# A matmul-tanh-multiply kernel: the loads of w's last column block are released by another cast

## The chip, the cores and the metric

One Trainium2 chip, one of its cores. The metric is the device time of one launch in microseconds (us). A profile of one execution is at hand for the kernel before: its span runs from the first to the last instruction of the program, and its own time is a little longer than the span.

## The reference

```python
batch, m, k, n = 16, 512, 1024, 768      # x: 16x512x1024, w1 and w2: 1024x768, all float32
y1 = np.matmul(x, w1)
y2 = np.matmul(x, w2)
return (np.tanh(y1) * y2).astype(np.float32)
```

## The kernel before

**Tiling.** The 8192 rows of x make 64 row tiles of 128 (called mt, 0 to 63). The contraction over 1024 is eight slices k of 128. The 2 x 768 columns of w1 and w2 are cut into three blocks of 512: block a is w1's first 512 columns, block g holds the last 256 columns of w1 and of w2 side by side, and block b is w2's first 512 columns. Every operand is float16 on TensorE (PE), accumulated in float32 in eight PSUM banks.

**Stages.** Row tiles 0 to 3, the head, are multiplied plainly: one matmul of 128x512 for each row tile, block and k (line 434, `mm`, operations m0a0 to m3b7; those of row tile 3 and block b are kept for the very end). The other 60 row tiles go in 20 triples, with a scheme that does with 15 products of four matmuls each (line 457, `product`, operations p0.i to p14.i of triple i) what would plainly take more, and that needs sums of pieces of w (line 416, `w_sum`, operations B5 to B48, on VectorE, DVE) and of x (line 425, `x_sum`, operations S3.i to S63.i, on DVE). The sums of w are made once, while the head is multiplied. Results leave PSUM through tanh on ScalarE (ACT) and a multiply on DVE (thg0 to thg3 and mug0 to mug3 for block g of the head).

**How w comes in.** Block a and block g are loaded as float32 into slots of `arena` (operations La0 to La7, and Lg00 to Lg31: two halves for each pair of k) and cast to float16 in `wh`: a by DVE (ca0 to ca7), g by ACT (cg0 to cg7; line 372 and 370, `copy`). Lg20 and Lg21 bring what cg2 and cg6 cast, Lg30 and Lg31 what cg3 and cg7 cast. All g loads are issued on SP's queue (q1 in the profile). Block b is loaded by POOL's queue (q0, line 363), which turns float32 into float16 on the way and needs no cast; these eight operations are cb0, cb4, cb1, cb5, cb2, cb6, cb3, cb7, in this order. Behind them on POOL come the loads of the row tiles 6, 4, 5, then 7, 8, 9 and so on (line 366, `load_x`, operations L6, L4, L5, L7 ...). Only eight of POOL's loads can be under way by their semaphores: the ninth, L6, waits until cb0 has landed, L4 until cb4 has, and so on.

**What sets the order.** A small planner inside the kernel (class `Planner`) is given every operation with its engines, an assumed duration, what it needs and a due time, and a list `lands` of times at which loads are assumed to land. It plays the program through once and writes down the order in which each engine shall issue its operations. That order is fixed in the program: an engine that meets an operation whose input is not there yet waits, and all that stands behind it on the engine waits too. The planner's times have no other effect. `lands` comes from `shared_landings`, which lets the queues (`rings`) share the bandwidth in equal parts from the moments given in the list.

**The gate.** POOL's first operation after its start-up is a copy of one column of a cast slice (line 497, `gate`). It does nothing but wait for that cast; the b loads stand behind it.

```python
    GATE = ("g", 0)
    ...
    op("gate", {"pool": 0.1}, 0.0, ["c%s%d" % GATE], gate, *GATE)
    for n, what in enumerate(late):
        op(f"c{what}", {"pool": 0.58}, 0.1 * n, [], load_w, "b", int(what[1]), issued=[f"c{late[n - 1]}" if n else "gate"], lands=lands[what])
```

Of the kernel before, what the change touches and what calls it, by code (L numbers as in the profile page):

```python
# [74 lines left out]
class Planner:  # L75
# [9 lines left out]
    def op(self, name, engines, due, needs, fn, *args, behind=(), issued=(), chains=(), xfer=0.0, latency=None, seeds=False,  # L85
           lands=None, hold=0.0):
        assert name not in self.ops, name
        self.ops[name] = dict(engines=engines, due=due, needs=[n for n in needs if n], behind=[n for n in behind if n], issued=[n for n in issued if n], fn=fn, args=args,
                              chains=chains, xfer=xfer, latency=latency, seeds=seeds, lands=lands, hold=hold)
        for c in chains:  # L90
            self.chains.setdefault(c, {"left": 0, "bank": None, "end": 0.0, "act": 0.0, "dve": 0.0})["left"] += 1
# [134 lines left out]
def shared_landings(rings, start, latency):  # L226
    now, left, place, landed = start, {}, [0] * len(rings), {}
    while any(p < len(r) for p, r in zip(place, rings)):
        active = [j for j, r in enumerate(rings) if place[j] < len(r) and r[place[j]][1] <= now]
        waiting = [r[place[j]][1] for j, r in enumerate(rings) if place[j] < len(r) and r[place[j]][1] > now]  # L230
        if not active:
            now = min(waiting)
            continue
        step = min([left.get(j, rings[j][place[j]][2]) * len(active) for j in active] + [t - now for t in waiting])
        now += step
        for j in active:
            left[j] = left.get(j, rings[j][place[j]][2]) - step / len(active)
            if left[j] < 1e-6:
                landed[rings[j][place[j]][0]] = now + latency[j]
                place[j] += 1  # L240
                del left[j]
    return landed
# [3 lines left out]
def kernel(  # L246
# [266 lines left out]
    for n, p in enumerate(LAST_ORDER.split()):  # L513
# [5 lines left out]
    XW, XX = 0.655, 1.4  # L519
    on_sp = "x00 x10 x20 x30 x01 x11 a4 a5 x21 a6 x31 a7".split() + [f"g{k}{t}" for k in range(KH) for t in range(2)]  # L520
    late = [f"b{k}" for s, k in slices if s == "b"]
    rows_in = (HEAD + 2, HEAD, HEAD + 1)
    GATE = ("g", 0)
    rings = [[(n, 0.75 + 0.3 * j, 0.75 if n[0] == "g" else 0.81 if n in ("x10", "x20", "x30") else XW) for j, n in enumerate(on_sp)],
             [(f"a{k}", 0.75 + 0.45 * k, 0.81 if k else XW) for k in range(4)], [(n, 17.6 + 0.6 * j, 0.66) for j, n in enumerate(late)] + [(f"x{mt}", 22.0 + 0.6 * j, XX) for j, mt in enumerate(rows_in)]]
    lands = shared_landings(rings, 1.0, (2.1, 2.1, 2.6))

    for k in range(4):
# [1 line left out]
    for n, what in enumerate(on_sp):  # L530
# [3 lines left out]
        else:  # L534
            s, k = what[0], int(what[1])
            j = slices.index((s, k))
            old = [slices[i - SLOTS] for i in range(j, j + 1 + (s == "g")) if i >= SLOTS]
            op(f"L{what}", {"sp": 0.05}, 0.1 * n - 100, [], load_w, s, k, int(what[2]) if s == "g" else None, issued=before,
               behind=[f"c{a}{b}" for a, b in old], lands=lands[what])
    op("gate", {"pool": 0.1}, 0.0, ["c%s%d" % GATE], gate, *GATE)  # L540
    for n, what in enumerate(late):
# [12 lines left out]
    for t in range(2):  # L554
        for k in range(KO):
            late = START + 32 + 8 * (t * KO + k)
# [61 lines left out]
    mt = HEAD - 1  # L618
# [57 lines left out]
    for i in range(TRIPLES):  # L676
# [10 lines left out]
        for o in C_OPS:  # L687
# [19 lines left out]
            mt = HEAD + 3 * i + r  # L707
            due = soonest[i, name] + LAST
            if kind in ("t", "th"):
                lo, n = (0, F) if kind == "t" else (F, G)  # L710
                op(f"{name}.{i}", {"act": 0.5 if n == F else 0.285}, due, needs, c_tanh, i, r, o[4], lo, n, o[5],
                   behind=reuse_out(mt) + ([f"{FIRST_READER[name]}.{i}"] if i == TRIPLES - 1 and name in FIRST_READER else []), chains=chains)
            else:
                lo, n, at = (0, F, 0) if kind == "m" else (F, G, G)
                op(f"{name}.{i}", {"dve": 0.6 if n == F else 0.335}, due + 1, needs, c_mul, i, r, o[4], lo, n, at, chains=chains)
                outs[mt].insert(0 if kind == "m" else 1, f"{name}.{i}")
    for mt in range(MT):
# [7 lines left out]
        late = [f"{('p0', 'p4', 'p12')[(mt - HEAD) % 3]}.{i + 1}"] if i < TRIPLES - 2 else []  # L725
# [144 lines left out]
```

## Time and profile before

| | us |
|---|---|
| median of three runs | 298.97 |
| the three runs | 298.97, 302.17, 298.88 |
| the profiled execution's own time | 299.0 |
| its span | 297.2 |
| PE busy in the span | 289.5 (97%) |
| DVE busy | 254.9 (86%) |
| ACT busy | 226.1 (76%) |
| POOL busy | 51.7 (17%) |

The profile's rows give for each group or moment the engine, the line of the kernel, the operation, the tile written and the tiles read. A share of the whole span says little here: the head of the kernel, some 33 us, is another program than the 20 triples after it, so the time is read by windows and by the timeline of each engine. A matmul of 128x512 is listed with 379 ns, but such matmuls are pipelined and follow each other in about 0.216 us, as the starts in the timeline show.

### The profile page before, as it was taken

How to read it: one execution, taken by the hardware profiler on the slowest of the kernel's cores; microseconds unless marked ns; L12 is line 12 of the kernel's file. 1: busy time of each engine (PE TensorE's matmuls, PEld its weight loads, DVE VectorE, ACT ScalarE, POOL GpSimd, SP SyncE). 2: the span in 40 equal slices, each digit the busy share in tenths (PEclk: the TensorE clock that was granted, in tenths of full speed). 3: DMA queues.
4: the chain of work that ended last, by engine and by line, in shares of the span. 5: the costliest groups of instructions: out<-in, count | busy, mean ns of one | idle time of the engine just before them, and what ended most of it. 6: DMA issues, size and time to landing. Idle time of an engine off the chain costs nothing. (4 is left out here: it accounts for less than half of the span.)

```text
span 297.2 us, 4671 instructions
## 1 busy us (share of the span) xinstructions
PE 289.5 (97%) x1385; PEld 133.4 (45%) x1385; DVE 254.9 (86%) x539; ACT 226.1 (76%) x454; POOL 51.7 (17%) x129
## 2 busy tenths in 40 slices
PE   7999999999999999999999999999999999999993
PEld 5444444444444444444444444444444444444442
DVE  1669999989999998979989899889889898988884
ACT  3577899699878879797797988768686776868451
POOL 0064036030112210303122121122020200000000
PEclk9999999999999999999999999999999999999999
DMA  6999999999999999999999999999999999741234
GB/s 230 387 298 198 173 158 216 192 166 197 193 238 217 252 228 270 270 171 306 183 220 199 226 292 218 283 278 251 165 279 113 271 85 270 229 161 52 108 140 164
DMA packets 84427, 63.51 MB, mean 214 GB/s; under 512 B 62768, under 2 KB 66608, under 8 KB 84400
## 3 DMA queue, kind: packets, MB, share of 16 engines
q1 hardware_dynamic: 73456, 44.71, 64.0%
q0 software_dynamic: 9792, 16.78, 38.0%
q10 hardware_dynamic: 1152, 1.70, 1.6%
q8 instruction: 11, 0.18, 0.3%
q14 instruction: 16, 0.13, 0.1%
HBM read 39.85 MB, written 25.17 MB: 219 GB/s over the span
## 5 line engine op out<-in xcount | busy, mean ns | idle before, releaser
L457 PE MATMUL bank<-b,early_x 128*128 128x512 f16 x640 | 148.3, 379 | 0.1
L457 PEld LDWEIGHTS <-early_x 128*128 128x128 f16 x800 | 78.2, 98 | 95.1 <-issue 0.7
L461 ACT ACTIVATE arena<-bank 128x512 f32<-128x512 f32 x100 | 59.1, 596 | 33.4 <-PE bank L457 33.3
L467 DVE TENSOR_TENSOR bank<-bank,arena 128x512 f32<-128x512 f32 x100 | 69.6, 696 | 15.5 <-ACT arena L461 7.3
L475 DVE TENSOR_TENSOR o<-o,bank 128x256 f32<-128x256 f32 (+1 forms) x120 | 63.2, 547 | 5.8 <-ACT o L470 5.5
L394 ACT ACTIVATE junk<-xh 128x1024 f16<-128x1024 f16 x60 | 63.3, 1055 | 0.1
L457 PEld LDWEIGHTS <-xT 128*128 128x128 f16 x400 | 39.0, 98 | 46.4
L457 PE MATMUL bank<-b,xT 128*128 128x512 f16 x240 | 58.3, 379 | 0.0
L494 POOL CAST held<-xT 128x1 f32<-128x1 f16 x54 | 15.1, 280 | 163.7 <-DMA xT<-xh 163.7
L470 ACT ACTIVATE o<-bank 128x256 f32<-128x256 f32 (+1 forms) x80 | 34.4, 437 | 12.0 <-DVE bank L467 7.1
L457 PE MATMUL bank<-wh,xT 128*128 128x512 f16 x160 | 41.1, 379 | 0.0
L457 PE MATMUL bank<-wh,early_x 128*128 128x512 f16 x160 | 40.9, 379 | 0.0
L366 POOL DMA_DIRECT2D xh<-in_x_dram x60 | 31.7, 528 | 16.0 <-issue 5.4
L425 DVE TENSOR_TENSOR early_x<-early_x,xT 128x512 f16<-128x512 f16 x80 | 33.5, 418 | 0.6
L461 ACT ACTIVATE bank<-bank 128x512 f32<-128x512 f32 x40 | 21.5, 575 | 7.2 <-DVE bank L467 6.6
L470 ACT ACTIVATE o<-arena 128x512 f32<-128x512 f32 x40 | 25.1, 627 | 1.0 <-DVE arena L467 1.0
L434 PE MATMUL bank<-wh,xT 128*128 128x512 f16 x72 | 18.4, 379 | 1.1 <-DVE wh L372 0.5
L425 DVE TENSOR_TENSOR early_x<-xT,early_x 128x512 f16<-128x512 f16 x40 | 16.7, 418 | 0.0
L425 DVE TENSOR_TENSOR early_x<-xT,xT 128x512 f16<-128x512 f16 x40 | 16.7, 417 | 0.0
L467 DVE TENSOR_TENSOR bank<-arena,bank 128x512 f32<-128x512 f32 x20 | 13.9, 695 | 3.2 <-ACT o L470 1.7
L467 DVE TENSOR_TENSOR arena<-bank,arena 128x512 f32<-128x512 f32 x20 | 13.7, 685 | 1.4 <-ACT arena L461 1.3
L467 DVE TENSOR_TENSOR arena<-arena,bank 128x512 f32<-128x512 f32 x20 | 13.6, 678 | 0.0
(49 smaller groups left out, 135.4 us busy)
## 6 DMA issues: line engine op xcount, KB each, us to landing
out_dram<-o SPq DMA_DIRECT2D x60, 384.0 KB, 5.4
xh<-in_x_dram POOLq DMA_DIRECT2D x60, 256.0 KB, 6.7
arena<-in_w_dram SPq DMA_DIRECT2D x12, 256.0 KB, 5.5
early_x<-in_x_dram SPq DMA_DIRECT2D x8, 256.0 KB, 5.0
arena<-in_w_dram ACTq DMA_DIRECT2D x4, 256.0 KB, 5.9
wh<-in_w_dram POOLq DMA_DIRECT2D x8, 128.0 KB, 5.7
xT<-xh SPq DMA_TRANSPOSE x57, 6.6
out_dram<-o SPq DMA_DIRECT2D x2, 256.0 KB, 2.8
```

Of the source, the lines that this page charges most:

```text
L366: pin(nc.gpsimd.dma_start(xh(mt), xf[mt]))
L394: pin(nc.scalar.activation(junk[:, :src.shape[-1]], src, ACT.Abs, scale=scale, accum_out=sums[:, column:column + 1]))
L425: pin(engine[e].tensor_tensor(x_operand(i, v), x_operand(i, a), x_operand(i, b), OP[how]))
L434: pin(nc.tensor.matmul(bank(chain)[:, :rhs.shape[-1]], xt(mt)[:, k, :], rhs, start=first, stop=k == KO - 1, skip_group_check=True))
L457: pin(nc.tensor.matmul(place(i, dst), x_operand(i, a)[:, k, :], w_rhs(b, k), start=begins and k == 0, stop=k == KH - 1, skip_group_check=T ...
L461: pin(nc.scalar.activation(place(i, dst), place(i, src), ACT.Copy, scale=float(sign)))
L467: pin(nc.vector.tensor_tensor(place(i, dst), a, b, ALU.add if signs == (1, 1) else ALU.subtract))
L470: pin(nc.scalar.activation(out_tile(HEAD + 3 * i + r)[:, lo:lo + n], place(i, src)[:, :n], ACT.Tanh, scale=float(sign)))
L475: pin(nc.vector.tensor_tensor(o, o, place(i, src)[:, at:at + n], ALU.mult))
L494: pin(nc.gpsimd.tensor_copy(held, xt(mt)[:, 0, :1]))
```

## The change

The gate copies a column of the last slice of block a (cast by DVE) where it copied a column of the first slice of block g (cast by ACT), so POOL may issue the loads of block b once that earlier cast is done. In the list of assumed landings the first b load moves from 17.6 to 16.0, so that the planner takes the b slices as landing earlier and the last g slices as landing later.

```diff
-    GATE = ("g", 0)
+    GATE = ("a", 7)
     rings = [[(n, 0.75 + 0.3 * j, 0.75 if n[0] == "g" else 0.81 if n in ("x10", "x20", "x30") else XW) for j, n in enumerate(on_sp)],
-             ... [(n, 17.6 + 0.6 * j, 0.66) for j, n in enumerate(late)] + ...
+             ... [(n, 16.0 + 0.6 * j, 0.66) for j, n in enumerate(late)] + ...
     lands = shared_landings(rings, 1.0, (2.1, 2.1, 2.6))
```

The order that the planner writes changes with it. On PE, from the 17th matmul of block g on:

```
before: ... m3g1 m3g5 | m0g2 m0g6 m1g2 m1g6 m2g2 m2g6 m3g2 m3g6 | m0b0 | m0g3 m1g3 m0g7 m1g7 m2g3 m2g7 m3g3 m3g7 | m1b0 m2b0 | b4 x3 | b1 x3 | m0b5 ...
after:  ... m3g1 m3g5 | m0b0 m1b0 m2b0 | m0g2 m1g2 m0g6 m1g6 m2g2 m2g6 m3g2 m3g6 | b4 x3 | b1 x3 | m0g3 m1g3 m0g7 m1g7 m2g3 m2g7 m3g3 m3g7 | m0b5 ...
```

From m0b5 on PE's order is the same in both. On ACT, the tanh of rows 2 and 3 (block a) go ahead of cg2 and cg6, and the absolute sums D1 and D2 go ahead of cg3 and of thg0. On DVE the sums of w are dealt out anew: after B45.2 comes B6.0, then B5.3, B24.0, B36.3, B26.0, mug0 to mug3, B24.2, B37.3, B26.2, B18.0, B18.2, B6.2, B29.0; the second half of B29 moves from before S3.0 to behind S3.1. A few operations of ACT and DVE up to the third triple change places too; behind them the order is the same on every engine. No operation is added or taken away.

More of the change, by code (lines that the diff above doesn't have):

```diff
@@ L522 @@
     rows_in = (HEAD + 2, HEAD, HEAD + 1)
-    GATE = ("g", 0)
+    GATE = ("a", 7)
     rings = [[(n, 0.75 + 0.3 * j, 0.75 if n[0] == "g" else 0.81 if n in ("x10", "x20", "x30") else XW) for j, n in enumerate(on_sp)],
-             [(f"a{k}", 0.75 + 0.45 * k, 0.81 if k else XW) for k in range(4)], [(n, 17.6 + 0.6 * j, 0.66) for j, n in enumerate(late)] + [(f"x{mt}", 22.0 + 0.6 * j, XX) for j, mt in enumerate(rows_in)]]
+             [(f"a{k}", 0.75 + 0.45 * k, 0.81 if k else XW) for k in range(4)], [(n, 16.0 + 0.6 * j, 0.66) for j, n in enumerate(late)] + [(f"x{mt}", 22.0 + 0.6 * j, XX) for j, mt in enumerate(rows_in)]]
     lands = shared_landings(rings, 1.0, (2.1, 2.1, 2.6))
```

## The prediction

> **What bounds the kernel now.** First, where PE, the busiest engine, has idle time: a table of stretches of the span, each row with the busy time and count of PE, PEld, DVE, ACT and POOL, then granted clock, DMA share and GB/s.
>
> ```profile
> 16.00:20.00 4.00, 3.92 (x19) 1.72 (x18) 2.93 (x8) 3.81 (x8) 3.13 (x7) 1.00 1.13 343
> 20.00:24.00 4.00, 3.59 (x17) 1.46 (x15) 2.83 (x8) 3.15 (x6) 2.64 (x6) 1.00 1.22 199
> 24.00:28.00 4.00, 4.00 (x20) 1.84 (x19) 4.00 (x10) 3.67 (x10) 2.15 (x5) 1.00 1.15 192
> ...
> 40.00:60.00 20.00, 20.00 (x95) 9.05 (x93) 19.83 (x43) 16.95 (x35) 5.87 (x10) 1.00 1.10 203
> 60.00:80.00 20.00, 20.00 (x94) 9.04 (x93) 18.02 (x39) 19.04 (x41) 3.51 (x9) 1.00 1.18 175
> ```
>
> From 36 us on PE is never idle in any row, so whatever delays it in the head moves the end by as much. The only sizeable hole behind the first microseconds is between 20 and 24. The timeline of PE shows it:
>
> ```profile
> 18.81 1.24 PE L434 MATMUL bank<-wh,xT 128*128 128x512 f16 x5
> 19.89 0.59 PE L434 MATMUL bank<-wh,xT_kept 128*128 128x512 f16 x2
> 20.32 1.46 PE L434 MATMUL bank<-wh,xT 128*128 128x512 f16 x6
> 21.62 0.59 PE L434 MATMUL bank<-wh,xT_kept 128*128 128x512 f16 x2
> 22.62 1.79 PE L434 MATMUL bank<-wh,xT 128*128 128x512 f16 x7 [0.41 <-DMA wh<-in_w_dram]
> 24.25 0.59 PE L434 MATMUL bank<-wh,xT_kept 128*128 128x512 f16 x2
> ```
>
> By its order these are m3g1 and m3g5 at 19.89, the eight matmuls of g2 and g6 from 20.32, and m0b0 at 22.62, held by the landing of the first b slice. Ten starts from 18.15 to 20.32 give 0.216 us a matmul. The next row of that view starts at 24.68 with m1b0. Seventeen matmuls from 20.32 need 3.67 us and took 4.36: 0.69 us are lost, and that is all an earlier b slice could win here. Then, when the b slices move: the timelines of SP and POOL.
>
> ```profile
> 10.29 4.70 SPq L358 DMA_DIRECT2D arena<-in_w_dram  x8
> ```
>
> ```profile
> 16.87 0.44 POOL L497 CAST held<-wh 128x1 f32<-128x1 f16 x1 [15.56 <-ACT wh L370]
> 17.25 4.37 POOL L363 DMA_DIRECT2D wh<-in_w_dram  x8
> 22.86 1.18 POOL L366 DMA_DIRECT2D xh<-in_x_dram  x2 [1.24 <-DMA wh<-in_w_dram]
> ```
>
> All g loads are issued by 14.99. The gate opens at 16.87, the b loads are issued from 17.25 on, and L6 waits for cb0's landing. Of what the queues moved between 17.9 and 19.4, and between 19.5 and 20.5 (queue: packets, MB, share of 16 engines):
>
> ```profile
> q1 hardware_dynamic: 539, 0.52, 109.5%
> ```
>
> ```profile
> q0 software_dynamic: 151, 0.15, 87.9%
> q1 hardware_dynamic: 97, 0.09, 27.8%
> ```
>
> In the first window the first b load is issued (17.25 to 17.92), yet not one packet of its queue moves; the DMA engines are full with g. Only when g runs out does b begin. The same is seen at 135.8 to 138.7, with a load of x issued by 135.77 and, ahead of it in time, a transpose and stores on SP:
>
> ```profile
> q1 hardware_dynamic: 1351, 1.07, 111.3%
> ```
>
> That load also waits 2.9 us, with no packet in between. But it is served before the rest of a store issued at 136.15. So the DMA engines serve the two queues here in the order of issue, not in turns.
>
> **The change part by part.** *The gate.* Its new cast, ca7, runs on DVE from 14.63 for 0.43 us, to 15.06. With the distances of before (gate 16.87, first issue 17.25 to 17.92) POOL issues cb0 from about 15.5 to 16.2, 1.75 us earlier. That is still behind the last g load (14.99). Served in the order of issue, b's packets begin when g's end, about 19.5 as before: g, b and then L6, L4, L5 land when they did (by the trace's record of each load: b0 about 22.6, b4 23.2, b1 23.9, b5 24.6; the last g half 22.1; L6, L4 and L5 28.39, 29.63 and 30.95). What stands behind the gate on POOL, eight b loads and the x loads, comes no earlier, since the DMA engines have no gap to fill and L6 still waits for cb0. Gain: nothing, the transfer time of g being the cover; if b did get in early the price changes (first rival).
>
> *PE's order.* m0b0 to m2b0 now stand ahead of g2 and g6. PE reaches m0b0 at 20.32 and waits until 22.62: 2.30 us. Eight ready matmuls of g2 and g6 are queued behind it and cannot cover that any more; this is the wait that the change adds. From 22.62 on nothing is late: m0g2 at 23.27 (its cast done about 20.85), m0b4 at 24.99 and m0b1 at 25.64 (landed 23.2, 23.9), m0g3 at 26.29 (cast from 22.2 on), so m0b5 comes 25 matmuls after 22.62, at 28.02. Before it came 8 after 24.68, at 26.41. So 2.30 takes the place of 0.69: **+1.61 us**. The transposes of L6, L4 and L5 (28.79, 30.10, 31.42 before, 0.4 us behind the landings) move by the same, farther from the landings.
>
> *ACT's order.* tha2 and tha3 ahead of cg2: cg2 comes from 19.24 to about 20.23, and DVE's B5.2 from 20.21 to about 20.9, B45.2's end from 21.88 to 22.6. D1 ahead of cg3 runs in ACT's wait up to 22.2. On the path: nothing, as PE stands until 22.62.
>
> *DVE's order.* B6.0 now comes first and waits for cb1 (23.94), with B5.3 and all else behind it: 23.99. By the rows of DVE (0.60 us for a sum of 128x1024 in a row of them, 0.33 for 128x512, 0.33 for a multiply at line 441): B6.0, B5.3, B24.0, B36.3, B26.0 to 26.55. mug0 waits for thg0, which waits for m0g7 (started 26.72, out 27.10): 27.45; mug3 waits for thg3 behind m3g7 (27.80) and ends about 28.9. Seven sums follow, six of 0.60 and one of 0.33, 3.93 together: S3.0 could start at 32.85. But S3.0 needs the evacuation of row 4, done at 31.59 before and 1.61 later now, 33.20. So all these waits of DVE lie beside PE's delay, with 0.35 us to spare; were that cover gone, they would count one for one.
>
> *The second half of B29* (0.60) ran before S3.0 in DVE's wait for row 4; now it runs behind S3.1, and DVE is 0.60 us further behind than PE is. What needs it later has slack at first (B27 is done at 38.2, the first product that reads it starts at 39.9). But from 40 to 60 DVE is busy 19.83 of 20 us, so only 0.17 is absorbed there: between 0 and 0.60 us of new PE waits; from 60 to 80 (18.02 of 20) the rest is made up. I take the middle, **+0.3**.
>
> Sum: 1.61 + 0.3 = 1.9. The profiled execution took 299.0 (span 297.2), the median 298.97, so no correction is needed: **300.9 us**, its own range 300.4 to 301.6.
>
> **A page against the trace.** The Trainium skill, "DMA: Bandwidth & Descriptors", section "Queues, rings and completion order", says that each DMA engine goes round robin between the queues it has work for, packet by packet. The rows at 17.9 and 135.8 disagree: 1.5 and 2.9 us without a turn for POOL's queue. By the page b would interleave with g, which is the first rival. The page "TensorE: Matmul & The Clock Gate", Part 1, lets the PE clock fall to half after an idle window of about 3.4 us; the 2.3 us wait is shorter, so by it the forecast stands and the third rival falls; no row of before shows an idle PE that long behind its start.
>
> **The rivals.** *1. The queues take turns after all*, now that b is issued while four g loads, not two, are unfinished. For it: nothing shows what a longer overlap does. Against it: the two windows. Load by load, b (0.66 us each by the landings, 0.65 apart) delays the last four g loads by 4 x 0.65 = 2.6: the last g half lands at 24.7, b0 before 20.3. PE takes m0b0 without a wait, reaches m0g3 at 20.32 + 17 x 0.216 = 23.99 and waits for cg3, 24.7 + 0.65 = 25.35: 1.36, and 0.1 for cg7, in place of 0.69: +0.8, with 0.2 for DVE: 300.0; between 299.2 and 300.6 by how evenly they share.
>
> *2. Faster.* As 1, but with g3 in time: if b0 lands by 20.3 and the last g half by 23.3 (cast by 23.99), PE loses nothing in the 0.69 and comes early. Its next wall is L6, landing at 28.39: the transpose moves from 28.79 to 28.43, so the gain is 0.36 and the time 298.6. For it: the planner's list assumes such landings. Against it: 8 halves of g and 3 b slices would have to pass in the time in which 8 halves of g did; the DMA share is over 1 all the while.
>
> *3. Slower: the clock.* In the 2.3 us wait PE's clock is taken back to half, as at the start, where 14 matmuls of 256 columns took 3.01 us and 5 of the same later 0.71. From the starts these are about 0.20 and 0.11 us each, for at least 3 us: half of that is lost, 1.5 us, making 302.4. It decides if the wait alone, not 3 us of idling, is enough. Against it: the granted clock is 1.00 in every row, though 0.41 us is the longest wait behind the start that they hold.
>
> *4. The change doesn't do what it says*: POOL starts no earlier, or earlier to no effect. The order is written by the planner either way, so the time is the forecast's.
>
> **How the numbers follow.** The forecast, with rival 4: 0.65; rival 1: 0.19; rival 2: 0.07; rival 3: 0.05; the DVE debt larger than 0.6: 0.04. The first two lie between 299.2 and 301.6; some room above for the last two gives a range of 299.1 to 301.9. Over 2%, about what a measurement of this kernel can tell from no change, would be 6 us, above 304.9 or below 293.0. No case reaches either: faster 0.01, within 0.97, slower 0.02.
>
> **What would show it.** In the profile after: gate at about 15.1 and b's issue from 15.5 (else rival 4); no packet of q0 before about 19.4 and b0 landing near 22.6; a single PE wait of about 2.1 to 2.3 us for wh<-in_w_dram ending at 22.6; the first transposes of line 384 after the head at 30.4 (28.79 before); then PE full, with at most 0.6 us of waits for DVE between 36 and 60. A b landing before 21.5, or an ACT wait for arena beyond 23, makes the first step wrong and a rival right; matmuls starting 0.4 us apart behind the wait would mean the clock.

## The result, and the profile after

The changed kernel takes 301.63 us in the median of 22 runs (300.19 to 308.04) against 298.97 (298.65 to 306.01): a ratio of 1.0074, 95% interval 1.0051 to 1.0096 (the ratio is taken without the few much longer runs that both kernels have). It is slower by 0.7%, less than the 2% of the verdicts, so "within 2%". Run again beside the later experiments it had 300.52 in the median of 12 runs, ratio 1.0046 (1.002 to 1.0072). The lowest runs of the first comparison lie 1.54 us apart (300.19 and 298.65); so even the fastest runs lose about that much; the rest of the median's 2.66 comes from some runs and not from others.

The profiled execution of the first comparison took 302.89 us (span 301.1). Its timeline of POOL:

```profile
15.06 0.18 POOL L497 CAST held<-wh 128x1 f32<-128x1 f16 x1 [13.75 <-DVE wh L372]
15.18 4.37 POOL L363 DMA_DIRECT2D wh<-in_w_dram  x8
22.52 0.53 POOL L366 DMA_DIRECT2D xh<-in_x_dram  x1 [2.97 <-DMA wh<-in_w_dram]
```

The change does what it says: the gate opens 1.8 us earlier than before (15.06 against 16.87) and the b loads are issued from 15.18 on (17.25 before). What the queues moved between 16.0 and 19.2:

```profile
q1 hardware_dynamic: 1155, 1.12, 110.2%
```

Not one packet of POOL's queue is among them, though its first load was issued by 15.84. The first b slice landed at 22.23 (before: 22.58), L6 at 28.13 (28.39). The timeline of PE, of the same execution:

```profile
19.82 0.59 PE L434 MATMUL bank<-wh,xT_kept 128*128 128x512 f16 x2
22.27 2.10 PE L434 MATMUL bank<-wh,xT 128*128 128x512 f16 x9 [1.85 <-DMA wh<-in_w_dram]
24.21 0.59 PE L434 MATMUL bank<-wh,xT_kept 128*128 128x512 f16 x2
...
30.04 0.61 PE L384 MATMUL bank<-ident_h,xh 128*128 128x128 f16 x8
```

m0b0 now follows m3g5 and waits for its slice; the eight matmuls of g2 and g6, which before lay in this time, come behind it. The transposes of L6 start at 30.04, where before had them at 28.79:

```profile
28.79 0.61 PE L384 MATMUL bank<-ident_h,xh 128*128 128x128 f16 x8
```

The five largest groups of waits of PE in the execution of the changed kernel, with the total, the number and the longest:

```profile
PE bank L457 <- ACT o L470: 1.9, 1, 1.9
PE bank L434 <- DMA wh<-in_w_dram: 1.9, 1, 1.9
PE bank L759 <- DVE ones L757: 1.1, 1, 1.1
PE bank L434 <- DVE wh L372: 0.5, 2, 0.3
PE bank L457 <- DVE o L475: 0.3, 1, 0.3
```

The first and the last line are new; these waits end at 224 and 54 us, far behind the head. The one at 224 goes back to DVE, which waited for a transposed row tile and was late from there on:

```profile
221.34 0.43 DVE L425 TENSOR_TENSOR early_x<-early_x,xT 128x512 f16<-128x512 f16 x1 [3.42 <-DMA xT<-xh]
```

The profiled execution of the second time (300.57 us) has neither; its largest groups are:

```profile
PE bank L434 <- DMA wh<-in_w_dram: 2.0, 1, 2.0
PE bank L759 <- DVE ones L757: 1.1, 1, 1.1
PE bank L434 <- DVE wh L372: 0.3, 1, 0.3
```

Its timeline of PE has the wait and, 1.56 later than before, the L6 transposes:

```profile
22.58 2.10 PE L434 MATMUL bank<-wh,xT 128*128 128x512 f16 x9 [1.96 <-DMA wh<-in_w_dram]
...
30.35 0.61 PE L384 MATMUL bank<-ident_h,xh 128*128 128x128 f16 x8
```

Its time is 1.57 above that of before's profiled execution. So the head accounts for the whole loss of that execution; what the other runs add has to come from elsewhere.

### The profile page after: what moved, and what is told of

Same layout as the page of the kernel before. It is cut to its first block, busy times and chain, and to the rows that moved or that the text cites. A ratio compares the mean times of both kernels' runs of the same rounds, so it can differ in the third digit from the quotient of the medians.

```text
span 301.1 us, 4670 instructions
## 1 busy us (share of the span) xinstructions
PE 290.2 (96%) x1385; PEld 133.6 (44%) x1385; DVE 254.9 (85%) x539; ACT 226.3 (75%) x454; POOL 50.7 (17%) x129
## 5 line engine op out<-in xcount | busy, mean ns | idle before, releaser
L470 ACT ACTIVATE o<-bank 128x256 f32<-128x256 f32 (+1 forms) x80 | 34.4, 437 | 13.8 <-DVE bank L467 8.7
L494 POOL CAST held<-xT 128x1 f32<-128x1 f16 x54 | 14.2, 262 | 173.4 <-DMA xT<-xh 173.4
L470 ACT ACTIVATE o<-arena 128x512 f32<-128x512 f32 x40 | 25.1, 628 | 1.0 <-DVE arena L467 1.0
```

The costliest lines, as they stand in the source:

```text
L470: pin(nc.scalar.activation(out_tile(HEAD + 3 * i + r)[:, lo:lo + n], place(i, src)[:, :n], ACT.Tanh, scale=float(sign)))
L494: pin(nc.gpsimd.tensor_copy(held, xt(mt)[:, 0, :1]))
```

## Which half of the change costs the time

The gate and the list of landings are independent edits. Theory: only the order that the list makes costs time, since POOL's loads are served behind the g loads in either case. Rival: the earlier gate crowds the last g loads.

**Gate alone.** The order on every engine is that of before.

```diff
-    GATE = ("g", 0)
+    GATE = ("a", 7)
     ... (n, 17.6 + 0.6 * j, 0.66) ...
```

> The gate of the changed kernel with the list of before: every engine's order is that of before, only POOL may issue b earlier. Theory (the DMA engines serve the loads in the order of issue, and all g loads are issued before the gate opens in either place): no change, lowest runs within 0.3 us of those of before; gate at 15.1, first packet of POOL's queue still at about 19.3 to 19.5, m0b0 at 22.3 to 22.6. Rival (the earlier gate itself costs time, by crowding the last g loads): the last g half lands later than 22.6 and the time is 0.8 us or more above before.

Measured: 299.27 in the median of 12 runs, lowest 298.83, beside 298.97 and 298.67; ratio 1.0000 (0.9975 to 1.0026). First packet of POOL's queue at 19.57, as the theory has it. But the last g half landed at 22.71 (22.12 before) and the first b slice at 22.26 (22.58): the two have changed places. The timeline of PE:

```profile
22.30 0.38 PE L434 MATMUL bank<-wh,xT 128*128 128x512 f16 x1
23.45 1.54 PE L434 MATMUL bank<-wh,xT 128*128 128x512 f16 x6 [0.78 <-ACT wh L370]
```

In the order of before m0b0 no longer waits, and m0g3 behind it waits 0.78 for its cast instead. In this execution the gate therefore cost about 0.6 (its L6 transposes start at 29.37); over the runs the effect is too small to be told from none.

**List alone.**

```diff
     GATE = ("g", 0)
-    ... (n, 17.6 + 0.6 * j, 0.66) ...
+    ... (n, 16.0 + 0.6 * j, 0.66) ...
```

> The list of the changed kernel with the gate of before: the engines' order is that of the changed kernel, b is issued from 17.25 as before. Theory (the order alone makes the loss): the time of the changed kernel, lowest runs 1.5 to 1.9 us above the lowest of before, one PE wait of about 2 us for the first b slice ending at 22.3 to 22.6. Rival (the gate): the time of before, within 0.3 us.

Measured: 302.05 in the median of 11 runs, lowest 300.18; ratio 1.0070 (1.0042 to 1.0098), the ratio of the whole change. The lowest run is 1.5 above before's. The order makes the loss. But the runs fall into two groups, five at 300.18 to 301.08 and five at 302.05 to 302.68, and the profiled one (302.68) belongs to the upper. Its stretches of the span show why (the column ahead of the last two is the granted clock):

```profile
22.00:24.00 2.00, 1.45 (x6) 0.63 (x6) 0.68 (x3) 2.00 (x5) 1.06 (x2) 0.87 1.24 202
24.00:26.00 2.00, 2.00 (x6) 0.68 (x5) 2.00 (x5) 0.41 (x2) 1.39 (x3) 0.50 1.20 208
26.00:28.00 2.00, 2.00 (x9) 0.84 (x8) 0.52 (x1) 0.00 (x0) 0.72 (x2) 0.78 1.12 208
```

and its timeline of PE:

```profile
22.55 3.14 PE L434 MATMUL bank<-wh,xT 128*128 128x512 f16 x9 [2.12 <-DMA wh<-in_w_dram]
...
32.00 0.61 PE L384 MATMUL bank<-ident_h,xh 128*128 128x128 f16 x8
```

Nine matmuls take 3.14 us behind a wait of 2.12, where the changed kernel's nine took 2.10. The clock was at half from 23.5 to 26.9 (3.4 us by the record of the clock), and the L6 transposes start at 32.00 instead of 30.35: 1.65 more. This is the third rival of the prediction.

**Three matmuls ahead**, in the kernel before, and nothing else; ACT, DVE and POOL keep their order.

```diff
     order = plan.run()
+    moved = ["m0b0", "m1b0", "m2b0"]
+    order = [n for n in order if n not in moved]
+    at = order.index("m0g2")
+    order[at:at] = moved
```

> Before, with one edit of the written order: m0b0, m1b0 and m2b0 are issued by PE ahead of g2 and g6, as in the changed kernel; ACT, DVE, POOL and the gate are as before. Theory (the wait of PE for the first b slice is the whole head loss): 1.6 us above before, first transposes of line 384 after the head at about 30.4. Rival (ACT's and DVE's new order makes it): at most 0.3 us above before.

Measured: 301.96 in the median of 12 runs, lowest 300.36; ratio 1.0062 (1.0031 to 1.0093). Three matmuls moved on one engine make the whole loss of the head; the new order of ACT and DVE is not needed for it. The profiled execution again waited 2.13 us for the b slice and had the clock at half for 3.4 us behind it (23.6 to 27.1), so that its L6 transposes start at 32.10 and not at the 30.4 that was expected:

```profile
22.65 3.07 PE L434 MATMUL bank<-wh,xT 128*128 128x512 f16 x9 [2.13 <-DMA wh<-in_w_dram]
...
32.10 0.61 PE L384 MATMUL bank<-ident_h,xh 128*128 128x128 f16 x8
```

**Three matmuls back**, in the changed kernel.

```diff
     order = plan.run()
+    moved = ["m0b0", "m1b0", "m2b0"]
+    order = [n for n in order if n not in moved]
+    at = order.index("m3g6") + 1
+    order[at:at] = moved
```

> The changed kernel, with those three matmuls put back behind m3g6; all else stays changed (gate, list, the order of ACT and DVE, b4 and b1 ahead of g3). Theory: PE waits about 0.4 to 0.6 us at m0b0 and reaches m0b5 near 26.4 as before, so the lowest runs come to within 0.5 us of the lowest of before (what is left is DVE's debt, 0 to 0.6). Rival (DVE's and ACT's order): the loss stays, 1.5 us above before.

Measured: 300.82 in the median of 12 runs, but five of them at 298.83 to 299.19; ratio 1.0017 (0.9976 to 1.0058). In its profiled execution the L6 transposes start 0.15 ahead of before:

```profile
28.64 0.61 PE L384 MATMUL bank<-ident_h,xh 128*128 128x128 f16 x8
```

So the head's loss is gone with gate, list, and the order of ACT and DVE still changed. The median is not back at before's: the profiled execution (303.32) was one of the kernel's long ones, with two waits behind the head, of 1.99 and 1.87 us, that were released by ACT's L470, as in the changed kernel's own profile.

## DVE's debt

The prediction put 0.3 us on the second half of B29, which runs later on DVE. Put back:

```diff
     order = plan.run()
+    order.remove("B29.2")
+    at = order.index("S3.0")
+    order[at:at] = ["B29.2"]
```

> The changed kernel, with the second half of B29 put back on DVE ahead of S3.0. Theory (DVE's debt makes the PE wait of 0.32 us near 54 us): that wait goes, and the lowest runs come 0.3 us down, to about 299.9. Rival (the debt is of no account): lowest runs as those of the changed kernel, 300.2.

Measured: 301.59 in the median of 6 runs, lowest 300.55; ratio 1.0110 (1.0062 to 1.0157). Nothing is won. The wait near 54 us is there, and longer (1.2 us), and DVE's timeline ahead of it says what is late:

```profile
50.28 0.41 DVE L425 TENSOR_TENSOR early_x<-early_x 128x512 f16<-128x512 f16 x1
51.97 0.42 DVE L425 TENSOR_TENSOR early_x<-early_x,xT 128x512 f16<-128x512 f16 x1 [1.27 <-DMA xT<-xh]
```

Here a transposed row tile is late, not DVE. In the changed kernel's first profile DVE waits for such tiles too; the listings of before and of the changed kernel's second profile have no such group between 40 and 290 us:

```profile
DVE early_x L425 <- DMA xT<-xh: 5.3, 4, 3.4
```

In that second profile, with the same order, there is no PE wait at all behind the head but one of 0.14. So the debt is not a cost of every execution. In the first profile the wait of 0.32 near 54 us has a late tile ahead of it as well, but DVE waited only 0.20 for that; whether B29 had a part in the rest is not shown.

## The clock

Theory: PE's wait of 2 us brings the clock to half in some executions, and that is the upper group near 302. Test: keep PE busy in the wait, with matmuls that are of no use and cost nothing there.

```diff
     order = plan.run()
+    plan.ops["fill"] = dict(fn=constants, args=(("b", 0), 12))
+    plan.engine_of["fill"] = "pe"
+    plan.start_of["fill"] = plan.start_of["m0b0"]
+    at = order.index("m0b0")
+    order[at:at] = ["fill"]
```

> The changed kernel, with 12 matmuls of constants (128x256, 0.11 us each, about 1.3 us; the kernel has the same ones at its start) issued by PE just ahead of m0b0, into the bank that m0b0 then begins anew. They lie in PE's wait for the first b slice, so they cost no time by themselves. Theory (the runs of the changed order fall into two groups, near 300.5 and near 302.1, because PE's 2 us of idling takes the clock to half for 3.4 us in some executions, which costs 1.7): the upper group goes, the median comes to 300.3 to 300.8, no row of the granted clock near 0.5 between 22 and 28. Rival (the upper group comes from late transposes of x): the two groups stay and the median is about 302.

Measured, in the changed kernel: 300.72 in the median of 6 runs, five at 300.25 to 301.05 and one at 307.22; ratio 1.0063 (1.0048 to 1.0077). PE's wait for the b slice is down to 0.3. Six runs are few, so the same again with a control, and with the gate of before, whose profiles had shown the half clock.

> The changed kernel once more, as the control of the next three on the same chip. Theory (PE's idling trips the clock in some executions): a third to a half of the runs near 302, the others 300.2 to 301.2. Rival (the upper group belongs to single late transposes of x): the same here, and the same in the next two.

> The changed kernel with the 12 matmuls of constants in PE's wait, once more for more runs. Theory (clock): the runs lie at 300.2 to 301.1, at most one or two beyond, median 0.5 us or more below the control's. Rival (late transposes): a third to a half near 302 as in the control.

> The same 12 matmuls of constants in the kernel with the changed list and the gate of before, whose profile had the clock at half for 3.4 us behind a wait of 2.12 us, and which had 5 of 11 runs near 302. Theory (clock): 300.2 to 301.1 in nearly all runs, granted clock 1.00 in all rows between 22 and 28. Rival: the same two groups as without them.

Measured: the control, 12 runs, had 300.52 in the median, eleven at 300.12 to 301.45 and one at 308.85: no group near 302. The changed kernel with the fill, 14 runs: 301.26 in the median, seven at 300.38 to 301.01, the others up to 307.91; ratio 1.0063 (1.0029 to 1.0098). It is not better than the control, and the expectation on these two fell. The control itself also missed what was expected of it, a third to a half of the runs near 302. The list alone with the fill, 12 runs: 300.44 in the median, nine at 300.16 to 300.56, two at 301.5, one at 307.33; ratio 1.0041 (1.0009 to 1.0072). Its granted clock:

```profile
22.00:24.00 2.00, 1.50 (x7) 0.68 (x7) 0.83 (x3) 2.00 (x5) 1.06 (x2) 1.00 1.24 203
24.00:26.00 2.00, 2.00 (x11) 0.92 (x10) 2.00 (x5) 0.52 (x2) 1.43 (x3) 1.00 1.20 208
```

With the gate of before and m0b0 ahead (list alone, three ahead) 9 of 23 runs lie between 301.8 and 302.7, and none of 12 with the fill. That alone does not show the clock: the runs with the fill are from another chip, with no runs of the list alone beside them, and on that chip the changed kernel had no group near 302 even without the fill.

The mean granted clock that is on record for each run says more. A stretch of 3.4 us at half takes 0.006 off the mean of a span of 300 us. The profiled executions with such a stretch have means of 0.993 and 0.994, all others 0.996 to 1.000. Of the nine runs between 301.8 and 302.7 five have 0.993 or 0.994; the other four have 0.996 to 1.000 and were not slowed by such a stretch. So the clock is about half of that group. Of the runs with the fill in this variant, the eleven under 302 all have 0.996 or more.

In the changed kernel the five runs between 301.8 and 302.9 among the first 22 have 0.996 to 1.000: that group is not the clock. The one of them that was profiled (302.89) is longer by the waits at 224 and 54 us; for the other four no profile exists. Three runs beyond it (303.16, 303.85, 304.25) have 0.990 to 0.994, so their clock was at half somewhere, but where in the span is not on record. The fill changes nothing in the changed kernel that can be measured.

## Can b be made early enough?

If b came as early as the list says, the new order would be right. The gate was put two casts of block a further ahead:

```diff
-    GATE = ("a", 7)
+    GATE = ("a", 5)
```

> The changed kernel (list and order) with the gate at a5's cast (about 12.3), so that b0 is issued from 12.5 and b0, b4, b1 ahead of the last g loads. Theory (served in the order of issue): first packets of POOL's queue at about 17.5, b0 lands by 19.5, no PE wait at m0b0, the last g half lands at 23 to 24 and PE waits 0 to 0.8 for its cast; lowest runs 298.7 to 299.5. Rival (SP's queue is always emptied first): first packets at 19.4, b0 at 22.3, the time of the changed kernel, 300.2 and more. Second rival (the queues take turns): b0 by 19.5 and the last g half later than 24.5, lowest runs 299.5 to 300.5.

Measured: 303.07 in the median of 6 runs, lowest 301.43; ratio 1.0141 (1.0106 to 1.0176). b0 was issued at 12.54, its first packet moved at 16.86 and it landed at 18.45. From 18 us on the two queues shared the DMA engines; what they moved between 18 and 22:

```profile
q0 software_dynamic: 522, 0.48, 70.8%
q1 hardware_dynamic: 519, 0.50, 45.3%
```

The packets are as good as equal in number, 522 to 519, as they would be in turns, and since POOL's take longer (70.8% against 45.3% of the engines' time) g gets less than half of that time. The last g half landed at 27.17 (22.12 before), and PE waits for g's casts:

```profile
PE bank L434 <- ACT wh L370: 3.4, 2, 2.5
```

That is the first rival of the prediction, in a stronger form than any of the expectations had it. A milder version puts the gate one cast of block a ahead and m0b0 to m2b0 back behind m3g6, to let b0 pass only the last g loads:

```diff
-    GATE = ("a", 7)
+    GATE = ("a", 6)
     order = plan.run()
+    ... (the three matmuls moved back, as above)
```

> An attempt at a better version: the order with m0b0, m1b0 and m2b0 put back behind m3g6 (b4 and b1 stay ahead of g3), and the gate at a6's cast (about 13.7), so that b0 is issued from about 13.9, just ahead of the last g loads. If b0 lands by 21.5 and the last g half by 23, PE has no wait in the head and the first transposes move to L6's landing: lowest runs 298.3 to 298.6, just below those of before (298.7). If the two queues take turns over more than the last g load, that half lands beyond 23.3, PE waits for cg3 and the lowest runs are 299.0 or more.

Measured: 299.53 in the median of 12 runs, lowest 299.02; ratio 1.0030 (1.0004 to 1.0055). b0 landed at 19.91, but the last two g halves at 22.23 and 24.40 (19.89 and 22.12 before): b0 was issued at 13.83, ahead of both (13.95 and 14.58), and the queues shared the engines over both. PE waits for casts twice, 0.40 and 0.39. It is not better than before. No version beat the kernel before.

## Why the prediction was right, and where it was not

- **The gate earns nothing.** Right, and for the reason given: 1155 packets of q1 and none of q0 between 16.0 and 19.2. The landings were not quite those of before: in the two profiles b0 came at 22.23 and 22.54 (22.6 foreseen) and the last g half at 22.56 and 22.69 (22.1 foreseen). In the order of before the later g half cost 0.6 in the one execution that was profiled; over the runs no cost can be told from none.
- **PE's order, +1.61.** The mechanism is right, and three matmuls alone bring the loss and take it away; the size is a little too large. The L6 transposes moved by 1.56 in the second profile (28.79 to 30.35) and by 1.25 in the first. Of the 1.56, 0.14 was there before the wait, as m3g1 started at 20.03 and not at 19.89; in the first profile it started 0.07 early. The wait itself thus cost 1.42 and 1.32. PE stood idle for 1.96 and 1.85, where the prediction's sign was 2.1 to 2.3; with the gate of before, where b0 landed about when it did before (22.51 and 22.61), it was 2.12 and 2.13. That the shift came out at 1.56 is in part luck.
- **ACT and DVE hidden beside it.** Right. In the first profile S3.0 starts at 32.88 behind a wait of 0.23 for ACT's evacuation of row 4, so DVE had 0.23 to spare (0.35 foreseen).
- **B29, +0.3.** Wrong. Moving it back won nothing, and an execution without that wait has it moved all the same. What stands behind the head instead differs between executions: 1.9 at 224 us behind a late row tile and 0.3 at 54 in one profile, nothing in the other.
- **The sum**, 300.9, lies between the two medians of the changed kernel (300.52 and 301.63), but for a partly wrong reason, and its closeness is in part luck: the certain part is about 1.5, no steady term of 0.3 was found behind it, and what brings the first median to 301.63 is that many runs are longer, some by later waits and a few by the clock. Why row tiles come late in some executions, and whether the change makes that more frequent, was not settled: before has runs up to 306 as well.
- **The rivals.** The sharing of the queues (first rival) does exist, as soon as g loads are issued behind b's; in this change, where all of g is issued ahead, no packet of b moved before 19.29. The clock (third rival) does strike behind a wait of 2.1 us, at 1.65 us (1.5 foreseen), in variants of the kernel; in the two profiles of the changed kernel it didn't, but only just, as the last section shows. The prediction gave this rival 0.05 and put the idling that is needed at 3 us at most; 2.04 us within one window of the clock were enough, and the first and second profile stayed below that with 1.71 and 1.96. That the rival stayed away there was luck. By the page "TensorE: Matmul & The Clock Gate", Part 1, of the Trainium skill, a wait under 3.4 us would not do; the runs show that 2.12 can.

## What to carry to other kernels

An earlier issue helps only if the DMA engines have something to give: look at whether they run out of packets before you expect a transfer to come sooner. An engine that works in a fixed order should be given first what is certain to be there; ready work behind a doubtful wait cannot cover it, and here three misplaced matmuls cost about 1.5 us. A table of assumed landings belongs next to the measured ones before it is turned.

## What the runs showed of the hardware that was not expected

- A load that joins from POOL's queue waited here for the loads that SP had begun to issue before it: 3.4 to 3.8 us from its issue to its first packet (issued by 15.84, 13.21 and 14.49 with the gates at a7, a5 and a6; first packets at 19.29, 16.86 and 18.24). With the gate at a5 only SP's queue moved packets between 13.2 and 16.8, 1217 of them. That is not the start of POOL's queue itself: in the kernel before, a POOL load issued by 37.7 had its first packet 0.7 us later. With SP loads issued after it, the queues moved packets in equal numbers (522 to 519). What in the DMA engines makes the difference was not tried.
- The clock's record falls into windows of 3.413 us. In every trace it begins at a moment of its own (3.8 to 6.7 us) and changes only at multiples of 3.413 us from there: in the run of the list alone it is full from 6.40 and at half from 23.47, five windows later. What decides is how long PE stood idle within one such window. Up to 290 us of the span, in all thirteen traces, the windows with the most idle time are these:

| execution | window, us | PE idle in it, us | next window |
|---|---|---|---|
| three ahead | 20.23 to 23.64 | 2.13 | half |
| list alone | 20.05 to 23.47 | 2.12 | half |
| changed kernel with the fill, second time | 186.49 to 189.90 | 2.04 | half |
| changed kernel, second time | 19.84 to 23.26 | 1.96 | full |
| three back | 196.28 to 199.69 | 1.87 | full |
| B29 put back | 19.20 to 22.61 | 1.79 | full |
| gate at a5 | 19.57 to 22.99 | 1.72 | full |
| changed kernel, first time | 18.71 to 22.13 | 1.71 | full |

The limit lies here between 1.96 and 2.04 us of idling in one window. A longer wait that is split between two windows passes: with the gate at a5 PE waited 2.52 us, 1.72 of it in one window and 0.79 in the next, and the clock stayed full. As the windows start at another moment in each execution, the same wait of 2.1 us falls into one window here and is split there. That fits the list alone and three ahead, which had the clock at half in some executions and not in others; for their runs without a profile it is not shown.
